# Gated embedding of a decoder layer: where the second half's operand sums stand, which engine adds the residual, and which PSUM banks take the transposes

## The chip, the cores and the metric

The kernel runs on one core of a Trainium2 chip. Its engines are TensorE (PE in the profile, with its weight loads as PEld), VectorE (DVE), ScalarE (ACT), GpSimd (POOL) and SyncE (SP), which here issues every transfer of tiles. The metric is the device time of one execution in microseconds. The trace is one profiled execution.

## The reference, cut to what matters

One layer of a decoder on a sequence of 2048 tokens of width 1024: two kinds of mixing, an output projection, a gated feed-forward part, and at the end a gated embedding. The change touches only the passage from the feed-forward part to the gated embedding and the gated embedding itself:

```
        y = (jax.nn.silu(gate) * up) @ w_down[i]
        h = h + rmsnorm(y, ffn_post_norm[i])
        h = h + (p[i] @ ple_proj[i]) * jax.nn.sigmoid(h @ ple_gate[i])
    return h
```

All arithmetic is float32. Each operand of a product is split into a rounded high part and a low rest, and each product is three matrix products of these (high by high, high by low, low by high).

## The kernel before, in words

The 2048 tokens are handled as four groups of 512 (g = 0 to 3) and, in the last part of the kernel, as two halves of two groups each. Six stages follow each other there: stage 0 `gate_up` of the first half, stage 1 `down` of the first half, stage 2 `gate_up` of the second half, stage 3 `down` of the second half, stage 4 `ple` (the gated embedding) of the first half, stage 5 `ple` of the second half. Every stage computes its matrix product by seven products of sums of blocks, taken in the order 1, 2, 6, 3, 7, 5, 4 (`CHAIN`); `chain` adds each product from its PSUM bank into running sums.

A `ple` stage has 36 steps. Steps 0 to 27 are the seven products of `h @ ple_gate`, four steps each (one for each 128 tokens), twelve matmuls of 512 columns a step. Steps 28 to 35 are `run_p`: for each 128 tokens and each half j of the columns, six matmuls give `p @ ple_proj`; ScalarE takes the sigmoid of the finished sums, VectorE multiplies (L1131), the residual is loaded (L1133) and added (L1134), and the result is stored (L1136).

`pair_of` splits an operand: ScalarE casts the high part (L811), GpSimd or VectorE subtracts it to get the low part (L812). The raw operand lies in one of 12 buffers (`wr`) that `load` (L796) takes in turn for everything. The weights of a step are prepared up to five steps ahead. `Drive` runs the steps in order, and after step i of stage a it calls the functions hung there with `at(a, i, ...)`:

- `s_part(1, ss1, part, k)`, k = 0 to 3, builds the operands of stage 5 from the transposed result. Part 0 makes the operands of products 1, 2 and 6. Part 1 makes those of products 4, 3, 7 and 5: four loads, four additions or subtractions on VectorE (L816, L819), four splits, of which two low parts are on GpSimd (products 4 and 5) and two on VectorE (3 and 7). In the kernel before, part 1 hangs after steps 26, 27, 28 and 29 of stage 4.
- `post_y(g, i)` normalises 128 rows of group g and adds the residual; `turn_y(g, i, tag)` transposes them with TensorE, four 128x128 blocks to a PSUM bank for each half j of the columns (L1086), copies the bank out with ScalarE (L1088) and stores it. Groups 0 and 2 turn in stages 1 and 3 with the tag "mm", groups 1 and 3 in stages 2 (after steps 2 to 5) and 4 (after steps 4 to 7) with the tag "hg".

The PSUM banks have five tags: "mm" has three banks, "z" two, "av", "tr" and "hg" one each. In stages 2, 4 and 5 the products take the tags in the order mm, z, mm, z, mm, av, tr; "hg" is not among them.

The order of TensorE's instructions is that of the program. The order on the other engines and on the transfer queue is made by a planner that simulates the program and takes what it finds ready, earlier program lines first; an engine then runs its own list strictly in order.

Of the kernel before, what the change touches and what calls it, by code (L numbers as in the profile page):

```python
# [89 lines left out]
def hybrid_block(  # L90
# [83 lines left out]
    def bank(tag):  # L174
        return ps.tile([P, 512], F32, tag=tag, name=tag, bufs=BANKS[tag])
# [4 lines left out]
    def mm_bank():  # L180
        mm_count[0] += 1
        return bank(mm_tags[mm_count[0] % len(mm_tags)])
# [40 lines left out]
    def mm3(o, l, r, start, stop):  # L223
        nc.tensor.matmul(o, l[0], r[0], start=start, stop=False)  # L224
        nc.tensor.matmul(o, l[0], r[1], start=False, stop=False)  # L225
        nc.tensor.matmul(o, l[1], r[0], start=False, stop=stop)  # L226

    def cut(pair, j):
        return pair[0][:, j * P:(j + 1) * P], pair[1][:, j * P:(j + 1) * P]
# [564 lines left out]
    def load(src, shape=None):  # L794
        r = slot("wr", 0, "wr")
        nc.sync.dma_start(r if shape is None else shape(r), src)  # L796
        return r

    def acc(name="acc"):
        turns["acc"] += 1  # L800
        return slot("acc", 0 if turns["acc"] % 3 == 0 else 1, name)

    def pair_of(src, kind, prod, lo_engine):
        if kind == "u":
            side = 0 if prod in (1, 2, 6) else 1
        else:
            turns["w"] += 1
            side = turns["w"] % 2
        hi = slot(kind + "h", side, kind + "h", F32R)
        lo = slot(kind + "l", side, kind + "l", F32R)  # L810
        nc.scalar.copy(hi, src)  # L811
        lo_engine.tensor_tensor(lo, src, hi.bitcast(F32), op=ALU.subtract)  # L812
        return hi, lo

    def sub(e, o, a, b):
        e.tensor_tensor(o, a, b, op=ALU.subtract)  # L816

    def add(e, o, a, b):
        e.tensor_tensor(o, a, b, op=ALU.add)  # L819

    V, G = nc.vector, nc.gpsimd
# [65 lines left out]
    def s_blk(grp, i, j, k):  # L887
        return load(h2t_s[2 * grp + i][4 * j + k])
# [15 lines left out]
    def s_part(grp, ss, part, k):  # L904

        a11, a12, a21, a22 = (s_blk(grp, i, j, k) for i, j in ((0, 0), (0, 1), (1, 0), (1, 1)))
        if part == 0:
            ss[1, k] = pair_of(a11, "u", 1, G)
            ss[2, k] = pair_of(a12, "u", 2, V)
            add(V, a21, a21, a22)  # L910
            sub(V, a21, a21, a11)
            ss[6, k] = pair_of(a21, "u", 6, V)
        else:
            ss[4, k] = pair_of(a22, "u", 4, G)
            add(V, a22, a21, a22)
            sub(V, a21, a11, a21)
            sub(V, a11, a22, a11)
            sub(V, a12, a12, a11)
            for prod, a, e in ((3, a12, V), (7, a21, V), (5, a22, G)):
                ss[prod, k] = pair_of(a, "u", prod, e)  # L920

    def chain(prod, c, b, new):

        if prod == 1:
            c["u"] = new("cu")
            nc.scalar.copy(c["u"], b)
        elif prod == 2:
            c[1, 1] = new("c11")
            add(V, c[1, 1], b, c["u"])
        elif prod == 6:  # L930
            add(V, c["u"], b, c["u"])
        elif prod == 3:
            c[1, 2] = new("c12")
            add(V, c[1, 2], b, c["u"])
        elif prod == 7:
            add(V, c["u"], b, c["u"])
        elif prod == 5:
            add(V, c[1, 2], b, c[1, 2])
            c[2, 2] = new("c22")
            add(V, c[2, 2], b, c["u"])  # L940
        else:
            c[2, 1] = c["u"]
            sub(V, c[2, 1], c["u"], b)
# [137 lines left out]
    def turn_y(g, i, tag):  # L1081

        for j, t in enumerate(ready[g][i]):
            b = bank(tag)
            for c in range(TT):
                nc.tensor.transpose(b[:, c * P:(c + 1) * P], t[:, c * P:(c + 1) * P], ident)  # L1086
            e = acc("ht")
            nc.scalar.copy(e, b)  # L1088
            nc.sync.dma_start(
                h2t_s[g][TT * j:TT * (j + 1), :, i * P:(i + 1) * P].rearrange("k p t -> p k t"),  # L1090
                e.rearrange("p (k t) -> p k t", k=TT))


    def ple(grp, ss):
        g0 = 2 * grp
        s = {}
        cs = [{} for _ in range(TT)]
        nk = ND // 2

        def prepare(prod):  # L1100
            w = []
            for k in range(nk):
                if prod in (1, 2, 3):
                    i, j = {1: (0, 0), 2: (1, 0), 3: (1, 1)}[prod]
                    r = (4 * i + k) * P
                    t = load(ple_gate[r:r + P, j * GT:(j + 1) * GT])
                else:
                    t = load(wp_s[k][{5: 1, 6: 2, 7: 3, 4: 4}[prod] - 1])
                w.append(pair_of(t, "w", 0, V if k % 2 else G))
            s[prod] = w  # L1110

        def run(prod, i):
            b = mm_bank()
            for k in range(nk):
                mm3(b, cut(ss[prod, k], i), s[prod][k], k == 0, k == nk - 1)
            chain(prod, cs[i], b, new_dn)

        def prepare_p(half):
            if half == 0:
                s["p"] = [[pair_of(load(ple_proj[k * P:(k + 1) * P, j * GT:(j + 1) * GT]), "w", 0, G)  # L1120
                           for k in range(2)] for j in range(2)]
            s["pt", half] = [pair_of(load(pt_s[g0 + half][k]), "w", 0, V) for k in range(2)]

        def run_p(half, i):
            for j in range(2):
                b = mm_bank()
                for k in range(2):
                    mm3(b, cut(s["pt", half][k], i), s["p"][j][k], k == 0, k == 1)
                y = cs[i][1 + half, 1 + j]
                nc.scalar.activation(y, y, AF.Sigmoid)  # L1130
                nc.vector.tensor_tensor(y, b, y, op=ALU.mult)  # L1131
                c = slice(j * GT, (j + 1) * GT)
                hr = load(h2_s[g0 + half][i * P:(i + 1) * P, c])  # L1133
                add(G, y, y, hr)  # L1134
                r0 = (g0 + half) * GT + i * P
                nc.sync.dma_start(out[r0:r0 + P, c], y)  # L1136

        def none():
            pass

        steps = []
        for pre, go, items in ((prepare, run, CHAIN), (prepare_p, run_p, range(2))):
            for it in items:
                for i in range(TT):
                    steps.append(((lambda pre=pre, it=it: pre(it)) if i == 0 else none,
                                  lambda go=go, it=it, i=i: go(it, i)))
        return steps
# [85 lines left out]
    tt0, tt1, ss0, ss1 = {}, {}, {}, {}  # L1233
# [51 lines left out]
    def at(stage, step, f):  # L1285
        hooks.setdefault((stage, step), []).append(f)
# [24 lines left out]
    for g in range(NG):  # L1311
        stage, step, every, lag, tag = (
            (1, 67, 2, 3, "mm"), (2, 0, 1, 2, "hg"), (3, 67, 2, 3, "mm"), (4, 0, 1, 4, "hg"))[g]
        for i in range(TT):
            at(stage, step + i * every, lambda g=g, i=i: post_y(g, i))
        for i in range(TT):
            at(stage, step + i * every + lag, lambda g=g, i=i, tag=tag: turn_y(g, i, tag))
    for k in range(ND // 2):
        at(4, 13 + 2 * k, lambda k=k: s_part(1, ss1, 0, k))
        at(4, 26 + k, lambda k=k: s_part(1, ss1, 1, k))  # L1320
    drive.run(hooks)


# [25 lines left out]
```

## Time and profile before

| | |
|---|---|
| time, median of 3 runs | 3057.65 us (3057.45 to 3063.77) |
| time of the profiled execution | 3053.19 us |
| span of the profiled execution | 3051.3 us |
| mean granted TensorE clock | 0.988 of full speed |
| busy share of the span | PE 96%, PEld 80%, DVE 68%, ACT 52%, POOL 48% |

The profiled execution's time is the span and 1.9 us around it. All times of the trace count from the start of the span. Stage 2 begins at about 2163 us, stage 4 at 2825 us, its steps 28 to 35 end at 2935.8 us where stage 5 begins, and the last matmul ends at 3046.3 us.

### The profile page before, as it was taken

The page shows a single profiled execution, that of the slowest core. Times are in us where ns is not written, and L with a number is a line of the kernel's source. Part 1 is how long each engine was busy: PE and PEld are TensorE (multiplying, and loading weights), DVE is VectorE, ACT ScalarE, POOL GpSimd, SP SyncE. Part 2 cuts the span into 40 slices and gives each one's busy share as a digit, 9 for nine tenths or more (in the row PEclk, how much of TensorE's full clock was granted, in tenths as well). Part 3 has the DMA queues.
Part 4 walks back from the last instruction along what each step waited for, and adds up shares of the span by engine and source line. Part 5 has one row for each costly group of instructions (what it writes and reads, how often), then busy time and mean ns, then how long its engine had stood idle before and what let it go on. Part 6 is the DMA issues. An engine that isn't in the chain of part 4 may idle for free.

```text
span 3051.3 us, 52890 instructions
## 1 busy us (share of the span) xinstructions
PE 2926.5 (96%) x18280; PEld 2431.2 (80%) x18280; DVE 2071.6 (68%) x2917; ACT 1582.7 (52%) x3188; POOL 1468.2 (48%) x1426
## 2 busy tenths in 40 slices
PE   8999899999999998898898999999999999999989
PEld 6888688878787787788786878888788888878767
DVE  3556566677676776765787787655777776656674
ACT  5666656666666666666523233455433333545442
POOL 3344445545556666867522322445722321457564
PEclk9999999999999999999999999999999999999999
DMA  7775565555545444457867867667955555677874
GB/s 218 220 211 163 151 178 162 149 154 163 151 130 158 144 136 134 153 190 256 285 209 242 265 210 249 224 199 216 342 178 169 173 172 173 210 217 247 308 248 138
DMA packets 469420, 602.28 MB, mean 197 GB/s; under 512 B 43168, under 2 KB 277664, under 8 KB 469152
## 3 DMA queue, kind: packets, MB, share of 16 engines
q1 hardware_dynamic: 469152, 598.91, 62.6%
q8 instruction: 144, 2.36, 0.3%
q14 instruction: 124, 1.02, 0.1%
HBM read 439.89 MB, written 158.86 MB: 196 GB/s over the span
## 4 chain that ended last, share of the span: by engine, by line
PE 43%; DVE 3%; DMA 3%; POOL 2%; issue 2%; ACT 1%; SPq 0%; POOLq 0%; DVEq 0%; ACTq 0%
PE mm L224 6%; PE mm L225 6%; PE mm L226 6%; PE z L226 4%; PE z L225 4%; PE z L224 4%; PE av L225 2%; PE av L226 2%; PE tr L224 2%; PE tr L225 2%; PE tr L226 2%; PE av L224 2%; DMA wr<-in_w_gate_up_dram 1%; DVE wl L812 1%; DVE wr L816 1%
## 5 line engine op out<-in xcount | busy, mean ns | idle before, releaser
L811 ACT CAST wh<-wr 128x512 fp32r<-128x512 f32 x600 | 352.1, 618 | 458.1 <-PE mm L225 159.9
L812 POOL TENSOR_TENSOR wl<-wr,wh 128x512 fp32r<-128x512 f32 x256 | 370.5, 1453 | 452.7 <-ACT wh L811 437.7
L435 POOL TENSOR_TENSOR a<-be,ring 128x512 f32<-128x512 f32 (+2 forms) x320 | 318.1, 994 | 436.0 <-DVE ring L431 418.9
L224 PE MATMUL mm<-uh,wh 128*128 128x512 f32 x1168 | 486.5, 417 | 3.5 <-DVE vv L350 2.0
L226 PE MATMUL mm<-uh,wl 128*128 128x512 f32 x1168 | 462.6, 396 | 0.0
L225 PE MATMUL mm<-ul,wh 128*128 128x512 f32 x1168 | 460.6, 394 | 0.0
L812 DVE TENSOR_TENSOR wl<-wr,wh 128x512 fp32r<-128x512 f32 x344 | 302.0, 885 | 182.9 <-ACT wh L811 172.5
L431 DVE TENSOR_TENSOR_SCAN ring<-z,ring,be 128x512 f32<-128x512 f32 x192 | 245.6, 1279 | 115.3 <-ACT z L417 112.3
L224 PE MATMUL mm<-wh,uh 128*128 128x256 f32 (+1 forms) x992 | 308.0, 310 | 0.0
L225 PE MATMUL mm<-wl,uh 128*128 128x256 f32 (+1 forms) x992 | 293.4, 296 | 6.9 <-POOL wl L812 6.9
L226 PE MATMUL mm<-wh,ul 128*128 128x256 f32 (+1 forms) x992 | 293.4, 296 | 0.0
L226 PEld LDWEIGHTS mm<-uh,wl 128*128 128x128 f32 x1168 | 221.5, 190 | 51.4
L224 PEld LDWEIGHTS mm<-uh,wh 128*128 128x128 f32 x1168 | 222.8, 191 | 46.2 <-issue 2.1
L225 PEld LDWEIGHTS mm<-ul,wh 128*128 128x128 f32 x1168 | 223.1, 191 | 39.9
L448 DVE TENSOR_TENSOR al<-tr,ah 128x512 fp32r<-128x512 f32 (+1 forms) x320 | 192.1, 600 | 90.7 <-ACT ah L446 90.0
L210 ACT CAST wh<-wr 128x512 fp32r<-128x512 f32 x288 | 178.3, 619 | 136.6 <-PE mm L225 80.8
L211 POOL TENSOR_TENSOR wl<-wr,wh 128x512 fp32r<-128x512 f32 x144 | 189.8, 1318 | 104.1 <-ACT wh L210 95.7
L812 POOL TENSOR_TENSOR wl<-s,wh 128x512 fp32r<-128x512 f32 x44 | 101.0, 2300 | 279.5 <-ACT wh L811 255.4
L446 ACT CAST ah<-tr 128x512 fp32r<-128x512 f32 (+1 forms) x320 | 167.5, 524 | 110.9 <-PE tr L443 108.2
L416 ACT ACTIVATE be<-z 128x512 f32<-128x512 f32 (+2 forms) x320 | 171.0, 534 | 88.2 <-PE z L410 38.5
L225 PEld LDWEIGHTS mm<-wl,uh 128*128 128x128 f32 x992 | 191.4, 193 | 12.5 <-POOL wl L812 7.4
L224 PEld LDWEIGHTS mm<-wh,uh 128*128 128x128 f32 x992 | 191.1, 193 | 7.9
(310 smaller groups left out, 7269.2 us busy)
## 6 DMA issues: line engine op xcount, KB each, us to landing
wr<-in_w_gate_up_dram SPq DMA_DIRECT2D x308, 256.0 KB, 3.8
wr<-in_w_in_dram SPq DMA_DIRECT2D x224, 256.0 KB, 3.2
wr<-hid_s SPq DMA_DIRECT2D x154, 256.0 KB, 3.1
wr<-in_w_down_dram SPq DMA_DIRECT2D x110, 256.0 KB, 3.4
hid_s<-hs SPq DMA_DIRECT2D x88, 256.0 KB, 3.7
wr<-wd_s SPq DMA_DIRECT2D x88, 256.0 KB, 3.1
kt<-k_s SPq DMA_DIRECT2D x80, 256.0 KB, 3.0
vt<-v_s SPq DMA_DIRECT2D x80, 256.0 KB, 3.3
```

Of the source, the lines that this page charges most:

```text
L210: nc.scalar.copy(hi, src)
L211: (lo_engine or nc.gpsimd).tensor_tensor(lo, src, hi.bitcast(F32), op=ALU.subtract)
L224: nc.tensor.matmul(o, l[0], r[0], start=start, stop=False)
L225: nc.tensor.matmul(o, l[0], r[1], start=False, stop=False)
L226: nc.tensor.matmul(o, l[1], r[0], start=False, stop=stop)
L416: nc.scalar.activation(be[:, :n], z[:, :n], AF.Sigmoid, scale=0.125)
L431: nc.vector.tensor_tensor_scan(r[:, o:o + n][:, ::-1], z[:, :n][:, ::-1], be[:, :n][:, ::-1], init, op0=ALU.mult, op1=ALU.bypass)
L435: nc.gpsimd.tensor_tensor(a[:, :n], be[:, :n], r[:, o + 1:o + n + 1], op=ALU.mult)
L446: nc.scalar.copy(hi[:, lo_c:], tr[:, lo_c:])
L448: nc.vector.tensor_tensor(lo[:, lo_c:], tr[:, lo_c:], hi[:, lo_c:].bitcast(F32), op=ALU.subtract)
L811: nc.scalar.copy(hi, src)
L812: lo_engine.tensor_tensor(lo, src, hi.bitcast(F32), op=ALU.subtract)
```

## The change

Three edits. `turn_y` takes the bank for the first half of the columns (j = 0) from the tag "mm" in every group, and only the second half uses the tag it was given; so groups 1 and 3 turn over an "mm" and the "hg" bank by turns, and nothing changes for groups 0 and 2. In `run_p` the residual of the first half of the columns (j = 0) is added on VectorE, that of the second stays on GpSimd. Part 1 of `s_part` for the second half is hung after steps 0, 2, 4 and 6 of stage 5 instead of steps 26 to 29 of stage 4.

```diff
     def turn_y(g, i, tag):
 
         for j, t in enumerate(ready[g][i]):
-            b = bank(tag)
+            b = bank(tag if j else "mm")
             for c in range(TT):
                 nc.tensor.transpose(b[:, c * P:(c + 1) * P], t[:, c * P:(c + 1) * P], ident)
...
                 hr = load(h2_s[g0 + half][i * P:(i + 1) * P, c])
-                add(G, y, y, hr)
+                add(G if j else V, y, y, hr)
...
     for k in range(ND // 2):
         at(4, 13 + 2 * k, lambda k=k: s_part(1, ss1, 0, k))
-        at(4, 26 + k, lambda k=k: s_part(1, ss1, 1, k))
+        at(5, 2 * k, lambda k=k: s_part(1, ss1, 1, k))
```

## Rows read from the trace of the kernel before

**Rows 1.** The page: busy us of each engine (share of the span).

```profile
PE 2926.5 (96%) x18280; PEld 2431.2 (80%) x18280; DVE 2071.6 (68%) x2917; ACT 1582.7 (52%) x3188; POOL 1468.2 (48%) x1426
```

**Rows 2.** Waits of PE from 2170 us on: total us, times, longest us.

```profile
PE hg L1086 <- ACT ht L1088: 7.1, 7, 2.5
PE mm L225 <- POOL wl L812: 6.9, 1, 6.9
PE mm L226 <- DVE wl L812: 2.4, 2, 2.1
...
PE hg L1086 <- POOL wl L812: 0.8, 1, 0.8
```

**Rows 3.** Timeline of PE, group 1 turned in stage 2: start us, us, instructions.

```profile
2180.15 0.60 PE L1086 MATMUL hg<-ident,cu 128*128 128x128 f32 x4
...
2181.90 0.47 PE L224 MATMUL z<-uh,wh 128*128 128x512 f32 x1
...
2202.32 0.60 PE L1086 MATMUL hg<-ident,cu 128*128 128x128 f32 x4
...
2205.79 0.47 PE L224 MATMUL mm<-uh,wh 128*128 128x512 f32 x1
2206.10 0.58 PE L225 MATMUL mm<-ul,wh 128*128 128x512 f32 x1
...
2209.75 0.39 PE L225 MATMUL mm<-ul,wh 128*128 128x512 f32 x1
2209.98 0.40 PE L226 MATMUL mm<-uh,wl 128*128 128x512 f32 x1
```

**Rows 4.** Timeline of PE: a turn of group 2 ("mm"), one of group 3 ("hg").

```profile
2803.45 1.04 PE L1086 MATMUL mm<-ident,c 128*128 128x128 f32 x8
2804.25 0.47 PE L224 MATMUL z<-wh 128*128 128x512 f32 x1
...
2838.97 0.60 PE L1086 MATMUL hg<-ident,cu 128*128 128x128 f32 x4
...
2840.72 0.48 PE L224 MATMUL mm<-wh,uh 128*128 128x512 f32 x1
```

**Rows 5.** Timeline of DVE in stage 2: the sum that frees an "mm" bank.

```profile
2187.00 0.68 DVE L819 TENSOR_TENSOR cu<-mm,cu 128x512 f32<-128x512 f32 x1
```

**Rows 6.** Timeline of PE in step 0 of stage 5.

```profile
2937.21 0.40 PE L224 MATMUL mm<-wh,uh 128*128 128x512 f32 x1
2944.55 0.79 PE L225 MATMUL mm<-wl,uh 128*128 128x512 f32 x1 [6.94 <-POOL wl L812]
...
2950.26 0.40 PE L226 MATMUL av<-wh,ul 128*128 128x512 f32 x1
```

**Rows 7.** Granted clock by stretch: PE, PEld, DVE, ACT, POOL busy; PEclk, DMA.

```profile
2945.00:2951.00 6.00, 6.00 (x17) 4.61 (x17) 1.03 (x2) 1.62 (x3) 6.00 (x5) 0.56 1.03 379
```

**Rows 8.** Timeline of POOL at the border of stages 4 and 5.

```profile
2934.80 2.99 POOL L819 TENSOR_TENSOR c<-c,wr 128x512 f32<-128x512 f32 x2 [0.68 <-DVE wr L819]
...
2942.78 1.72 POOL L812 TENSOR_TENSOR wl<-wr,wh 128x512 fp32r<-128x512 f32 x1
```

**Rows 9.** Groups of DVE from 2896 to 2945 us: busy us, mean ns.

```profile
L812 DVE TENSOR_TENSOR ul<-wr,uh 128x512 fp32r<-128x512 f32 x8 | 11.5, 1457 | 0.5 <-ACT uh L811 0.4
L816 DVE TENSOR_TENSOR wr<-wr 128x512 f32<-128x512 f32 x12 | 11.4, 952 | 0.1
L812 DVE TENSOR_TENSOR wl<-wr,wh 128x512 fp32r<-128x512 f32 x6 | 5.0, 846 | 0.0
L819 DVE TENSOR_TENSOR wr<-wr 128x512 f32<-128x512 f32 x4 | 3.8, 950 | 4.9 <-POOL ul L812 4.9
```

**Rows 10.** Timeline of DVE: the first sum of part 1.

```profile
2896.75 0.69 DVE L819 TENSOR_TENSOR wr<-wr 128x512 f32<-128x512 f32 x1 [2.80 <-POOL ul L812]
```

**Rows 11.** Timelines at the end: the last matmul of PE, POOL's last add.

```profile
3045.87 0.39 PE L226 MATMUL av<-wh,wl 128*128 128x512 f32 x1
...
3047.07 1.26 POOL L819 TENSOR_TENSOR c<-c,wr 128x512 f32<-128x512 f32 x1
```

## Prediction

> **What bounds the kernel now.** I read the page first, then the waits of PE, then PE's timeline around each wait. TensorE is busy for 96% of the span [rows 1], so time comes off only where TensorE stands still or works slowly. The waits of PE from stage 2 on show where it stands [rows 2]. Three of them lie in the places that the diff touches: it waits for ScalarE's copy of a transposed bank (7.1 us in seven turns, and 0.8 us in the eighth, where the profile names GpSimd but the place is the same), for one low part of a weight on GpSimd (6.9 us, once), and for a low part on VectorE (2.4 us) at the first steps of `run_p`. Each is small against 3000 us, and with TensorE full everywhere else a microsecond taken from one of them should reach the end.
>
> **The transposes.** In groups 1 and 3 both halves of the columns use the single "hg" bank: four transposes, then TensorE waits until ScalarE has emptied it, then four more. In group 1 a turn takes 1.75 us from its first transpose to the next matmul, and the last one 3.47 us [rows 3]; the other two of group 1 are like the first. In group 3 it is 1.75 us each [rows 4]. Group 2 turns over several "mm" banks, eight transposes without a stop, and takes 0.80 us [rows 4]. The changed code gives the two halves two different banks, so I price a turn at 0.80 us. Group 1: 3 x 1.75 + 3.47 - 4 x 0.80 = 5.5 us. Group 3: 4 x (1.75 - 0.80) = 3.8 us. The number of transposes and copies stays.
>
> The long stop of 3.47 us has a second price. After it nine matmuls take from 2206.10 to 2209.75, 3.65 us, where the following one shows 0.23 us for each [rows 3]: 3.65 - 9 x 0.23 = 1.6 us. It looks like the lower of TensorE's two clock levels, as the granted clock shows at the border below. Without the stop this should go: 1.6 us.
>
> What it adds is a wait for an "mm" bank. There are three, the products use three of every seven tags on them, and four more tenants come in. Behind a waiting transpose stands every later matmul. The one place where I find the bank late is the second turn of group 1: VectorE frees the bank of the third step at 2187.00 + 0.68 = 2187.7 us [rows 5], and the second turn, due at about 2187.5 us now (5.6 us after 2181.90, two products on), would come 0.95 us earlier, at 2186.6. If the banks go strictly round, that costs 1.1 us; if the free one is taken, nothing. The bounds for all eight turns are 0 and 8 x 1.1; I take 1.1 us, since in stage 4 VectorE is not behind and I find no late bank there.
>
> **The border of stages 4 and 5.** In the first step of stage 5 TensorE waits 6.9 us for the low part of the third weight, on GpSimd [rows 6]. GpSimd was not idle: from 2934.80 us it ran five residual adds, and the low part came behind them at 2942.78 us [rows 8]. These adds were late because VectorE was: from 2896 to 2945 us it spent 11.4 + 3.8 us on the 16 sums of part 1 and 11.5 us on their eight low parts, 26.7 of 49 us [rows 9], and the products that GpSimd was to add to stood between them. The change takes both away: the 26.7 us go to stage 5, and 8 of the 16 adds of each half leave GpSimd. VectorE gets 8 adds at 0.69 to 0.95 us [rows 9, 10], at most 8 us in place of the 26.7. GpSimd then has one add of at most 1.7 us [rows 8] for each 2.8 us step, so it should meet the weight in time: 6.9 us go. After the stop, 13 matmuls take from 2944.55 to 2950.26, 5.71 us [rows 6]; at 0.23 us they would take 3.0. The granted clock of that stretch is 0.56 of full [rows 7], mostly the lower level. Without the stop another 2.7 us go.
>
> The 2.4 us that TensorE waits for VectorE at the start of `run_p` [rows 2] are for the low parts of `p`, which stood among the same sums. With these gone I count 2.4 us; bounds 0 and 2.4.
>
> **What moves into stage 5.** All of part 1 goes with its 16 loads, 16 casts, 16 sums and 16 low parts. On the transfer queue the loads move past the residual loads and the stores of stage 4's `run_p`, and stand among the weights of products 6 and 3. Its first result is needed at step 12 (product 3), and all four k are needed there. A step is 12 x 0.23 = 2.8 us, so from the end of step 0, behind which the first sum is written, there are 11 steps or 30.4 us. VectorE's list for that stretch: part 1 at its old lengths 26.7 us, less the last low part of product 7 (1.46), eight sums of products 2 and 6 at 0.68 us [rows 5] = 5.4, six low parts of weights at 0.85 us [rows 9] = 5.1; together 35.8 us. That is 5.4 us too much if nothing starts early. But the planner takes work early where an engine is free: the first sum of part 1 ran at 2896.75 us [rows 10], while the step behind which it is written ended some ten steps of 2.8 us before 2937, at about 2909. In the changed stage 4 a `run_p` step leaves VectorE 2.8 - 2 x 0.68 - 0.8 = 0.6 us free, some 5 us over eight steps. So the operands come just in time or slightly late; I take 1 us, with bounds 0 and 5.4 + 2.7 for a stop long enough to lower the clock.
>
> A new wait sits inside this: the first sum of each k may overwrite its input only after GpSimd has made the low part of product 4, 2.80 us in the row [rows 10]. Behind it on VectorE stand the sums that free PSUM banks. A product's bank comes round after at least two steps, 5.6 us, so one such wait does not reach TensorE.
>
> A rule speaks against both moves. By the Trainium skill, "SBUF — State Buffer", section "Who interferes with whom", a VectorE instruction with two SBUF inputs and a GpSimd instruction that reads SBUF exclude each other for the whole instruction. The rows agree that there is a price: the sums of part 1 mean 0.95 us beside GpSimd's work, and 0.69 us for the first one [rows 9, 10]; what full exclusion would cost is a rival below.
>
> **The end.** The last matmul ends at 3046.3 us and GpSimd's last add starts at 3047.07 [rows 11]. It belongs to the second half of the columns and stays on GpSimd, so the tail is unchanged. If VectorE's add of the first half falls beside it, it takes 1.72 instead of 1.26 us [rows 8, 11]: 0 to +0.5 us, I take 0. The eight adds that VectorE now makes in stage 5 lie under matmuls: VectorE needs 2 x 0.68 + 0.8 = 2.2 us of a step's 2.8; if that cover went, it would be 8 x 0.7 us.
>
> **Sum.** Gains 5.5 + 3.8 + 1.6 + 6.9 + 2.7 + 2.4 = 22.9 us; losses 1.1 + 1.0. Net 20.8 us. Against the profiled execution's own 3053.19 us (span 3051.3 and 1.9 around it) that is 3032.4; the median of the runs lies 4.5 us above that execution, and from it the forecast is 3057.65 - 20.8 = 3037 us.
>
> **Rivals.**
> 1. VectorE late in stage 5. For it: the list of 35.8 us in 30.4, and the VectorE wait of [rows 10]. Against it: the free time before. If nothing starts early, 5.4 us of stop and 2.7 of clock: 22.9 - 1.1 - 8.1 = 13.7 us gained, 3044 us.
> 2. The border's stop survives, because GpSimd still has eight adds and part 1's first low parts may be drawn ahead of the weight. It keeps 9.6 us: 20.8 - 9.6 = 11.2 gained, 3046 us. Against it: what fed the queue, VectorE's 26.7 us, has left.
> 3. Full exclusion of VectorE and GpSimd. Alone, VectorE's list of stage 5 is 38 instructions (24 of part 1, eight sums, six low parts) at 0.68 us = 25.8 us; GpSimd's 14 low parts (eight of part 1, six of weights) at 1.26 us add 17.6. 43.4 against 30.4 us is 13 us of stop and 2.7 of clock: 22.9 - 1.1 - 15.7 = 6 us gained, 3052 us, about no change. This is what the rule of the Trainium skill ("SBUF — State Buffer") would give. Against it: 0.95 us is far below 0.68 + 1.26. The same result comes if the planner's new order opens stops elsewhere.
> 4. Slower: the raw buffers. Part 1 needs 16 loads, and the 12 `wr` buffers are shared with the weights taken ahead. If the planner loads the weights of products 6 and 3 first, part 1 runs only from the end of step 7, four steps or 11 us before it is needed, and before it was spread over 48 us [rows 9, 10]. 48 - 11 = 37 us of stop and 2.7 of clock against 21.8 gained: 18 us slower, 3076 us. It decides from a stop of 19 us on. Against it: the casts of those weights free their buffers as the earlier products finish, and part 1's first three k are written before the weights of product 3.
>
> **How the numbers follow.** Forecast 0.52; rival 1 0.20; rival 2 0.12; rival 3 and other new orders 0.09; rival 4 0.07. A change of 0.2% (6 us) is about what a measurement of this kernel can tell from none. The first three are faster by more than that: 0.84; rival 3 is the same: 0.09; rival 4 slower: 0.07. The forecast's own range is 3033 to 3041 from the bounds above (0 and 2.2 us of loss, 0 or 2.4 for `p`); the runs' scatter, 4.5 us down to the profiled one, takes its lower end to 3029. With rivals 1 and 2 the upper end is 3049, which leaves 0.16 out.
>
> **What would show it.** Right: turns of groups 1 and 3 in 0.8 us; no PE wait for L1088; no stop at the first step of stage 5 and no stretch of 0.43 us matmuls behind it; last add 2 us after the last matmul. Wrong: a PE wait at step 12 of stage 5 for a low part on VectorE (rival 1 or 3, by its length), a PE wait for GpSimd in step 0 (rival 2), loads of the second half's operands issued only after step 7 (rival 4), transposes waiting for VectorE (the banks).

## The result, and the profile after

The kernel after takes 3042.06 us (median of 4 runs, 3038.41 to 3045.58), the kernel before, in the same comparison, 3059.99 us (median of 4, 3057.45 to 3063.77). The ratio is 0.995 with a 95% interval of 0.9932 to 0.9967: 15 us faster, 10 to 21 by the interval (the two medians lie 17.9 us apart). The forecast was 3037 us in a range of 3029 to 3049. The profiled execution took 3042.35 us with a span of 3040.5 us.

The page of the kernel after, busy us of each engine, answers to [rows 1]:

```profile
PE 2925.5 (96%) x18280; PEld 2431.2 (80%) x18280; DVE 2082.0 (68%) x2933; ACT 1580.9 (52%) x3188; POOL 1459.0 (48%) x1410
```

VectorE has the sixteen residual sums that GpSimd has lost (x2933 for x2917, x1410 for x1426). Otherwise no engine has more or less to do, and what changed are the waits. The waits of PE of the kernel after from 2170 us on (total us, times, longest us) answer to [rows 2]:

```profile
PE mm L224 <- ACT uh L811: 9.6, 2, 9.1
PE z L226 <- DVE wl L812: 1.4, 1, 1.4
PE mm L1086 <- POOL c L819: 1.2, 1, 1.2
PE hg L1086 <- POOL c L819: 0.5, 1, 0.5
```

All three waits of [rows 2] on which the forecast rested are gone: the one for ScalarE's copy of the bank, the 6.9 us for GpSimd, the one for the low parts of `p`. One stands there that was not in the kernel before: 9.6 us for a high part from ScalarE.

The order of TensorE's instructions is the same in both kernels, so the path can be cut at the same instructions and the parts compared. The cuts, in the timeline of PE of the kernel after (start us, us, instruction): the first transpose of group 0, the first of group 1, the matmul behind group 1's last turn, the first transpose of group 2, the matmul behind group 3's last turn, `run_p` of stage 4, stage 5, its step 12, its step 14, its `run_p`, the last matmul.

```profile
2141.96 1.03 PE L1086 MATMUL mm<-ident,c 128*128 128x128 f32 x8
2178.81 0.60 PE L1086 MATMUL mm<-ident,cu 128*128 128x128 f32 x4
2199.66 0.48 PE L224 MATMUL mm<-uh,wh 128*128 128x512 f32 x1
2795.69 1.04 PE L1086 MATMUL mm<-ident,c 128*128 128x128 f32 x8
2843.31 0.47 PE L224 MATMUL z<-wh,uh 128*128 128x512 f32 x1
2899.11 0.40 PE L224 MATMUL mm<-wh 128*128 128x512 f32 x1
2921.59 0.39 PE L224 MATMUL mm<-wh,uh 128*128 128x512 f32 x1
2955.01 0.40 PE L224 MATMUL mm<-wh,uh 128*128 128x512 f32 x1
2973.79 0.39 PE L224 MATMUL mm<-wh,uh 128*128 128x512 f32 x1
3012.78 0.39 PE L224 MATMUL mm<-wh 128*128 128x512 f32 x1
3035.02 0.39 PE L226 MATMUL av<-wh,wl 128*128 128x512 f32 x1
```

Differences of these starts, and the same differences in the kernel before, whose cuts start at 2143.29, 2180.15, 2205.79, 2803.45, 2854.62, 2910.43, 2935.82, 2979.04, 2984.61, 3023.63 and 3045.87 us:

| stretch | before, us | after, us | change |
|---|---|---|---|
| group 0 to group 1 | 36.86 | 36.85 | 0.0 |
| turns of group 1 (stage 2) | 25.64 | 20.85 | -4.8 |
| from there to group 2 | 597.66 | 596.03 | -1.6 |
| groups 2 and 3 (stages 3, 4) | 51.17 | 47.62 | -3.6 |
| to `run_p` of stage 4 | 55.81 | 55.80 | 0.0 |
| `run_p` of stage 4 | 25.39 | 22.48 | -2.9 |
| stage 5, steps 0 to 11 | 43.22 | 33.42 | -9.8 |
| stage 5, steps 12 and 13 | 5.57 | 18.78 | +13.2 |
| stage 5, steps 14 to 27 | 39.02 | 38.99 | 0.0 |
| its `run_p` to the last matmul | 22.24 | 22.24 | 0.0 |
| all | 902.58 | 893.06 | -9.5 |

So between the two profiled executions the changed passage gave 9.5 us, not the 20.8 of the forecast: 22.7 us came off and 13.2 were put back in two steps. Another 1.3 us lie in the code ahead of group 0's transposes, which the change does not touch and in which every engine runs the same list: it ends at 2143.3 us in the one profiled execution and at 2142.0 in the other, and in the twelve other traces of this study, in which it is the same too, between 2143.9 and 2151.5. The ratio of whole runs carries this scatter. That it makes up all the rest of the 15 us is not shown, as the other executions left no trace; the same two kernels measured again (below) differ by 6 us, 2 to 10. The cut times are free of that scatter, and I rest on them below, but each is of one execution.

The turns, in the timeline of PE of the kernel after, answer to [rows 3] and [rows 4]: the first two of group 1, and the first of group 3.

```profile
2178.81 0.60 PE L1086 MATMUL mm<-ident,cu 128*128 128x128 f32 x4
2179.95 0.66 PE L1086 MATMUL hg<-ident,c 128*128 128x128 f32 x4 [0.54 <-POOL c L819]
2180.36 0.47 PE L224 MATMUL z<-uh,wh 128*128 128x512 f32 x1
...
2186.01 0.60 PE L1086 MATMUL mm<-ident,cu 128*128 128x128 f32 x4
...
2186.80 0.48 PE L224 MATMUL z<-uh,wh 128*128 128x512 f32 x1
...
2831.56 0.60 PE L1086 MATMUL mm<-ident,cu 128*128 128x128 f32 x4
2832.35 0.48 PE L224 MATMUL mm<-wh,uh 128*128 128x512 f32 x1
```

A turn takes 0.79 us in both groups (2186.80 - 2186.01, 2832.35 - 2831.56), but for the very first, where the second half waits 0.54 us for the residual sum on GpSimd. No transpose waits for a bank: the second turn starts at 2186.01 and goes through. VectorE ends the third step's sum, which frees the "mm" bank that the forecast expected to be late, only at 2186.2.

The new stop, in the timeline of PE of the kernel after, is in step 12 of stage 5, the first of product 3:

```profile
2957.15 0.50 PE L224 MATMUL mm<-wh,uh 128*128 128x512 f32 x1 [0.58 <-ACT uh L811]
...
2967.43 0.79 PE L224 MATMUL mm<-wh,uh 128*128 128x512 f32 x1 [9.05 <-ACT uh L811]
...
2973.14 0.58 PE L225 MATMUL z<-wl,uh 128*128 128x512 f32 x1
```

Behind it 13 matmuls take from 2967.43 to 2973.14, 5.71 us: the very stretch that stood behind the stop of [rows 6], 2.7 us more than at full pace. The granted clock over it, in the windows of the kernel after (busy us of PE, PEld, DVE, ACT, POOL; clock, DMA share, GB/s), is 0.50, the lower of the two levels, as it is in the kernel before over the same stretch (2944.55 to 2950.26 us; the 0.56 of [rows 7] takes in 0.75 us behind it):

```profile
2968.00:2973.00 5.00, 5.00 (x13) 3.87 (x12) 1.40 (x3) 0.42 (x1) 1.35 (x1) 0.50 0.62 201
```

ScalarE is only the last link. Its timeline in the kernel after shows the sixteen casts of part 1 in five bundles, and what it waited for:

```profile
2927.84 0.62 ACT L811 CAST uh<-wr 128x512 fp32r<-128x512 f32 x1
...
2933.93 2.18 ACT L811 CAST uh<-wr 128x512 fp32r<-128x512 f32 x4
...
2944.95 2.18 ACT L811 CAST uh<-wr 128x512 fp32r<-128x512 f32 x4
...
2956.48 2.18 ACT L811 CAST uh<-wr 128x512 fp32r<-128x512 f32 x4 [3.67 <-DVE wr L816]
...
2966.76 1.66 ACT L811 CAST uh<-wr 128x512 fp32r<-128x512 f32 x3 [6.02 <-DVE wr L816]
```

A bundle of four is products 3, 7 and 5 of one set and product 4 of the next. The last bundle waits 6.02 us for the sums of the fourth set on VectorE. The timeline of DVE of the kernel after, first sum of each set and the last sums:

```profile
2929.86 0.69 DVE L819 TENSOR_TENSOR wr<-wr 128x512 f32<-128x512 f32 x1 [1.88 <-POOL ul L812]
...
2941.59 0.68 DVE L819 TENSOR_TENSOR wr<-wr 128x512 f32<-128x512 f32 x1
...
2951.41 0.68 DVE L819 TENSOR_TENSOR wr<-wr 128x512 f32<-128x512 f32 x1
...
2961.26 1.74 DVE L819 TENSOR_TENSOR wr<-wr 128x512 f32<-128x512 f32 x1
2962.93 1.75 DVE L812 TENSOR_TENSOR wl<-wr,wh 128x512 fp32r<-128x512 f32 x1
2964.60 2.13 DVE L816 TENSOR_TENSOR wr<-wr 128x512 f32<-128x512 f32 x3
```

The sets start 10 to 12 us apart, although they are written two steps, 5.6 us, apart. The fourth ends at 2964.60 + 2.13 = 2966.73 us; step 12 stands at 2955.01. The experiments ask why.

### The profile page after: what moved, and what is told of

It reads as the page before. It is cut to its first block, busy times and chain, and to the rows that moved or that the text cites. A ratio compares the mean times of both kernels' runs of the same rounds, so it can differ in the third digit from the quotient of the medians.

```text
span 3040.5 us, 52870 instructions
## 1 busy us (share of the span) xinstructions
PE 2925.5 (96%) x18280; PEld 2431.2 (80%) x18280; DVE 2082.0 (68%) x2933; ACT 1580.9 (52%) x3188; POOL 1459.0 (48%) x1410
## 4 chain that ended last, share of the span: by engine, by line
PE 40%; issue 4%; DVE 3%; DMA 3%; POOL 3%; ACT 1%; SPq 0%; POOLq 0%; DVEq 0%; ACTq 0%
PE mm L224 5%; PE mm L225 5%; PE mm L226 5%; PE z L226 4%; PE z L225 4%; PE z L224 4%; PE av L225 2%; PE av L224 2%; PE av L226 2%; PE tr L224 2%; PE tr L226 2%; PE tr L225 2%; POOL wl L812 1%; DVE wl L812 1%; DMA wr<-in_w_gate_up_dram 1%
## 5 line engine op out<-in xcount | busy, mean ns | idle before, releaser
L226 PEld LDWEIGHTS mm<-uh,wl 128*128 128x128 f32 x1168 | 220.6, 189 | 51.3 <-POOL wl L211 0.3
L224 PEld LDWEIGHTS mm<-wh,uh 128*128 128x128 f32 x992 | 192.5, 194 | 18.4 <-ACT uh L811 10.4
```

## The experiments

Each table row below is the same cut of a profiled execution as above: the turns of group 1, groups 2 and 3, `run_p` of stage 4, steps 0 to 11 and steps 12 and 13 of stage 5, and all from group 0's first transpose to the last matmul, in us. The ratio is that of whole runs to the runs of the kernel before beside them, with its 95% interval.

| kernel | group 1 | groups 2, 3 | `run_p` | 0 to 11 | 12, 13 | all | ratio |
|---|---|---|---|---|---|---|---|
| before | 25.6 | 51.2 | 25.4 | 43.2 | 5.6 | 902.6 | 1 |
| after | 20.9 | 47.6 | 22.5 | 33.4 | 18.8 | 893.1 | 0.995 (0.9932 to 0.9967) |
| banks alone | 21.1 | 48.6 | 26.9 | 39.7 | 5.6 | 893.1 | 0.9968 (0.9958 to 0.9979) |
| residual sums alone | 24.9 | 51.3 | 25.6 | 42.5 | 5.6 | 900.0 | 1.0003 (0.9992 to 1.0014) |
| operand sums alone | 25.3 | 51.3 | 22.5 | 33.8 | 17.6 | 900.9 | 0.9992 (0.9979 to 1.0004) |
| banks and residual sums | 21.1 | 47.7 | 27.0 | 41.1 | 5.6 | 894.3 | 0.9985 (0.9976 to 0.9995) |
| after, once more | 21.0 | 48.4 | 22.5 | 33.4 | 18.4 | 894.1 | 0.998 (0.9967 to 0.9992) |
| product 7's low part on GpSimd | 21.0 | 47.4 | 22.5 | 33.4 | 18.9 | 893.5 | 0.9975 (0.9961 to 0.9989) |
| product 4's low part on VectorE | 21.1 | 47.5 | 22.5 | 33.4 | 16.5 | 891.0 | 0.9965 (0.9953 to 0.9978) |
| part 1 half a stage earlier | 20.8 | 47.4 | 22.5 | 45.3 | 5.6 | 892.0 | 0.9966 (0.9954 to 0.9977) |
| first sum into its own buffer | 21.2 | 48.5 | 22.5 | 33.4 | 8.3 | 883.8 | 0.9955 (0.9937 to 0.9973) |
| and product 4 split last | 21.1 | 48.3 | 22.5 | 33.4 | 8.0 | 886.0 | 0.9954 (0.9939 to 0.9969) |
| product 4's operand apart | 21.0 | 47.3 | 22.5 | 33.4 | 5.6 | 881.0 | 0.9931 (0.9907 to 0.9955) |
| that, residual sums on GpSimd | 21.1 | 47.3 | 22.5 | 33.8 | 5.6 | 880.8 | 0.9927 (0.9914 to 0.9941) |

### The three edits, one by one

**Banks alone.** The kernel before with

```diff
-            b = bank(tag)
+            b = bank(tag if j else "mm")
```

> Only the banks of the transposes are changed. My theory (the three edits act on separate stops): the eight turns of groups 1 and 3 fall from 1.75 to 3.5 us to 0.8 us, and the 1.6 us of slow matmuls in stage 2 go: 9 to 11 us faster, with the 6.9 us stop at the border of stages 4 and 5 unchanged. Rival (time won early is lost again at the next full engine): the border stop grows by what the turns give, and the kernel is faster by less than 4 us.

The two rows of turns fall by 4.6 and 2.5 us, and the kernel is 9.4 us faster by the cut times and 10 by the ratio, as expected. The stop at the border did not stay as it was: with nothing edited there, the waits of PE of this kernel show 3.3 us, half of its 6.9 us [rows 2].

```profile
PE mm L225 <- POOL wl L812: 3.3, 1, 3.3
```

Little of that is a gain. Steps 0 to 11 are 3.6 us shorter, but `run_p` is 1.5 us longer and the stretch ahead of it 0.9 (56.7 for 55.8): over the whole border, 1.2 us. TensorE comes earlier and waits at other places. The 0.9 are mostly a wait of 0.8 us for a high part from ScalarE ahead of the first matmul of `run_p`. In `run_p` the wait for VectorE is as long as before (2.3 us for 2.4), but behind it the granted clock falls: 0.66 from 2911 to 2916 us, where the kernel before shows 1.00 from 2911 to 2918.

**Residual sums alone.** The kernel before with

```diff
-                add(G, y, y, hr)
+                add(G if j else V, y, y, hr)
```

> Only the residual adds of the first half of the columns go to VectorE. My theory (VectorE, with 26.7 us of part 1 between its products, is what makes GpSimd's adds late): VectorE gets eight more instructions in the same stretch, so the border stop stays within 3 us of its 6.9 us; between 4 us faster and 4 us slower. Rival (GpSimd's queue of adds is the cause): with half the adds gone the low part of the weight is in time, the stop and the slow matmuls behind it vanish, 8 to 10 us faster.

The waits of PE of this kernel: the one stop has become two, and `p` is as late as before.

```profile
PE mm L225 <- POOL wl L812: 2.9, 1, 2.9
PE mm L226 <- DVE wl L812: 2.6, 2, 2.4
PE mm L225 <- DVE wl L812: 2.3, 1, 2.3
```

`run_p` and steps 0 to 11 together go from 68.6 to 68.1 us. By itself this edit moves the lateness from GpSimd to VectorE and gives nothing that runs can tell.

**Operand sums alone.** The kernel before with

```diff
-        at(4, 26 + k, lambda k=k: s_part(1, ss1, 1, k))
+        at(5, 2 * k, lambda k=k: s_part(1, ss1, 1, k))
```

> Only part 1 of the operand sums is moved to stage 5. My theory: the border stop and the 2.4 us wait for the low parts of p go (12 us with the slow matmuls), and the stop at product 3 of stage 5 seen in the changed kernel (9.6 us and 2.5 us of slow matmuls) comes: between 3 us faster and 3 us slower. Rival (the stop at product 3 comes from VectorE's extra adds or from the shifted arrival of TensorE, not from the sums): no stop at product 3, 10 to 12 us faster.

The border is as in the kernel after, 22.5 and 33.8 us: this edit alone takes both the stop and the wait for `p`, 12.3 us. And this edit alone makes the stop at product 3, as the waits of PE of this kernel show:

```profile
PE mm L224 <- ACT uh L811: 9.0, 1, 9.0
```

12.0 us are given back in steps 12 and 13. The edit as it stands is worth 0.3 us.

**Banks and residual sums**, the first two edits together.

> Banks and adds are changed, part 1 stays in stage 4. My theory: no stop at product 3 of stage 5; the turns give 9 to 11 us and the border stop stays in about the size that the adds alone leave it. Rival (GpSimd's queue is the cause of the border stop): 18 to 21 us faster than before, thus faster than the changed kernel.

The turns are as with the banks alone. Over the border (56.9 + 27.0 + 41.1 us for 55.8 + 25.4 + 43.2) it is 0.5 us slower than before. While the operand sums are in stage 4, the border as a whole moves by 1.2 us at most. By the ratio of whole runs this kernel gains 5 us and the banks alone 10, while their passages differ by 1.1 us; the rest of that difference is not explained.

### The stop at product 3: how long the list, or in what order?

**The kernel after once more**, beside the next three.

> The changed kernel once more, beside the next three. Expected as before: 12 to 18 us faster than the kernel before, with a stop of 8 to 11 us at product 3 of stage 5, before which TensorE waits for the cast of the fourth operand, and one stretch of slow matmuls behind it. If the stop is an accident of one execution, it is absent here.

The stop is 9.6 us again, with 18.4 us in steps 12 and 13: no accident of one execution. Its ratio, 0.998, means 6 us (2 to 10), below the 12 to 18 expected and below the 15 of the first comparison. Its cut time from group 0 on is only 1.0 us longer: the passage is worth 8.5 to 9.5 us, and the two ratios, from 4 and from 10 runs of the kernel after, lie on either side of that.

**Product 7's low part on GpSimd**: four instructions fewer on VectorE between the border and product 3.

```diff
-            for prod, a, e in ((3, a12, V), (7, a21, V), (5, a22, G)):
+            for prod, a, e in ((3, a12, V), (7, a21, G), (5, a22, G)):
```

> As the changed kernel, but the four low parts for product 7 are made on GpSimd instead of VectorE. Theory 1 (VectorE's list before step 12 is too long): three to four instructions of 0.7 to 1.7 us leave it, the stop at product 3 falls from 9.6 to 4 to 6 us; 3 to 6 us faster than the changed kernel. Theory 2 (VectorE waits in the chain from ScalarE's cast over GpSimd's low part for product 4 to the first sum, and is not full): GpSimd has four more instructions in that chain, the stop stays or grows by up to 5 us.

The stop is 10.5 us (the waits of PE of this kernel):

```profile
PE mm L224 <- ACT uh L811: 10.5, 2, 9.5
```

Taking work from VectorE did not shorten it. That speaks against a list too long for its time as the only cause, but the four low parts went to GpSimd, which the other theory has in the chain, so it does not decide between them.

**Product 4's low part on VectorE**: four instructions more there, and no wait for GpSimd ahead of the first sum.

```diff
-            ss[4, k] = pair_of(a22, "u", 4, G)
+            ss[4, k] = pair_of(a22, "u", 4, V)
```

> As the changed kernel, but the four low parts for product 4 are made on VectorE instead of GpSimd, so the first sum of each k no longer waits for GpSimd. Theory 1 (VectorE's list is too long): four instructions more, the stop at product 3 grows by 2 to 6 us. Theory 2 (the chain over GpSimd makes it late): the stop shrinks by 3 us or more.

The stop is 8.3 us, against 9.6 (the waits of PE of this kernel):

```profile
PE mm L224 <- ACT uh L811: 8.3, 1, 8.3
```

More work on VectorE, and 1.3 us less of a stop. That is not what a list too long would do, but it is less than the 3 us or more that the removal of the wait on GpSimd was to bring. It settled neither.

**Part 1 half a stage earlier**: its four parts hung after steps 30, 32 and 34 of stage 4 and step 0 of stage 5.

```diff
-        at(5, 2 * k, lambda k=k: s_part(1, ss1, 1, k))
+        at(*((4, 30), (4, 32), (4, 34), (5, 0))[k], lambda k=k: s_part(1, ss1, 1, k))
```

> As the changed kernel, but part 1 of the four sets hangs after steps 30, 32 and 34 of stage 4 and step 0 of stage 5. Theory 1 (VectorE's list between the end of step 0 and step 12 is too long): some 14 us more of time, the stop at product 3 vanishes; with the residual adds halved the border stop stays below 3 us: 8 to 13 us faster than the changed kernel. Rival (any sums in stage 4 bring the border stop back, whatever their number): a stop of 3 to 7 us for a weight's low part in step 0 of stage 5, within 5 us of the changed kernel.

Nothing stands at product 3, but steps 0 to 11 take 45.3 us, more than before the change. The waits of PE of this kernel name low parts of weights on both engines:

```profile
PE z L225 <- DVE wl L812: 4.0, 2, 2.7
PE mm L225 <- POOL wl L812: 2.0, 1, 2.0
```

The place in the program shifts the stop; it does not remove it. The passage is 1.1 us shorter than in the kernel after; the rival had said within 5 us.

### Cutting the chain

What these leave is a chain of orders. In the in-place sums, the first writes `a22 + a21` over `a22`, which product 4's split still reads. So in each set: ScalarE's cast for product 4, GpSimd's low part, the first sum, three more sums, the casts for products 3, 7 and 5, and behind these, in ScalarE's list, the next set's cast for product 4. The bundles above show it. For the fourth set in the kernel after: product 4's cast ends at 2956.48 + 2.18 = 2958.66; GpSimd's low part follows, in its timeline:

```profile
2958.22 2.57 POOL L812 TENSOR_TENSOR ul<-wr,uh 128x512 fp32r<-128x512 f32 x2 [4.25 <-ACT uh L811]
```

It ends at 2960.79, and the first sum starts at 2961.26; the last ends at 2966.73, and ScalarE casts at 2966.76. Some 10 us for one round, with what VectorE does in between (the weight's low part at 2962.93), four rounds in a row: from 2927.84, the first cast, to 2966.76 are 38.9 us, and from the border to step 12 there are 33.4.

**First sum into its own buffer.** The kernel after with a raw buffer more for each set; VectorE's list keeps its length.

```diff
-            add(V, a22, a21, a22)
+            add(V, n := slot("wr", 0, "wr"), a21, a22)
             sub(V, a21, a11, a21)
-            sub(V, a11, a22, a11)
+            sub(V, a11, n, a11)
             sub(V, a12, a12, a11)
-            for prod, a, e in ((3, a12, V), (7, a21, V), (5, a22, G)):
+            for prod, a, e in ((3, a12, V), (7, a21, V), (5, n, G)):
```

> The changed kernel, but the first sum of each set of part 1 is written to a raw buffer of its own, so that it need not wait until GpSimd has made the low part of product 4. VectorE's list keeps its length and ScalarE's casts their program order. Theory 1 (the list of VectorE between the border and product 3 is too long): the stop at product 3 stays at 8 to 10 us. Theory 3 (a chain in each set, cast of product 4, its low part on GpSimd, the first sum, the casts of products 3, 7 and 5, then the next set, some 10 us each and four of them in a row): the sums of the four sets start close together, the stop is gone or at most 3 us, and the kernel is 9 to 12 us faster than the changed one.

The waits of PE of this kernel:

```profile
PE mm L225 <- POOL wl L812: 0.7, 1, 0.7
PE mm L224 <- ACT uh L811: 0.5, 1, 0.5
```

The stop is 0.5 us, and 0.7 us for a weight beside it; steps 12 and 13 take 8.3 us for 18.8, with small gaps only. VectorE had the same instructions to do as in the kernel after, so 10.5 of the 13.2 us came from the one buffer that is written over. What is left goes with a full list. The windows from the border to the end of the last sum, of the kernel after and of this kernel (busy us of PE, PEld, DVE, ACT, POOL; clock, DMA share, GB/s):

```profile
2921.59:2966.73 45.14, 36.20 (x154) 28.43 (x152) 38.89 (x41) 19.79 (x36) 25.14 (x17) 0.92 0.70 234
2927.64:2964.39 36.75, 35.98 (x154) 28.35 (x152) 35.77 (x36) 17.29 (x32) 23.95 (x15) 1.00 0.73 243
```

In the kernel after VectorE is busy for 38.9 of 45.1 us and idle for 6.2. Here it is idle for 1.0, and three low parts of weights have moved behind the last sum. It has no room left, and the last sum still ends 3.3 us behind the place of step 12 (36.75 - 33.43). Nor do the four sets start close together, as theory 3 had it: their first sums start 6, 12, 23 and 28 us behind the border.

**And product 4 split last**, so that ScalarE casts for products 3, 7 and 5 first. As above, with

```diff
-            ss[4, k] = pair_of(a22, "u", 4, G)
...
-            for prod, a, e in ((3, a12, V), (7, a21, V), (5, n, G)):
+            for prod, a, e in ((3, a12, V), (7, a21, V), (5, n, G), (4, a22, G)):
```

> As the run with the sum's own buffer, and the split for product 4 is written last in each set, so that ScalarE casts for products 3, 7 and 5 first. Theory 1: a stop of 8 to 10 us as in the changed kernel. Theory 3 with the overwritten buffer as the only link of the chain: the same as with the own buffer alone, within 1 us. Theory 3 with ScalarE's order as a second link: the stop is at least 1 us shorter than with the own buffer alone, or is gone where that one still shows 1 to 3 us.

8.0 us in steps 12 and 13, the same within 0.3: the stop for ScalarE is 0.5 us in both. Once the buffer is free, ScalarE's order costs nothing more. (This execution is 2.2 us longer from group 0 to group 1, which has nothing to do with the edit; that is why its sum, 886.0, stands above that of the run before it.)

**Product 4's operand apart.** Part 1 makes only the sums and products 3, 7 and 5; product 4's block is loaded once more and split later.

```diff
-            ss[4, k] = pair_of(a22, "u", 4, G)
...
         at(5, 2 * k, lambda k=k: s_part(1, ss1, 1, k))
+        at(5, 8 + 2 * k, lambda k=k: ss1.update({(4, k): pair_of(s_blk(1, 1, 1, k), "u", 4, G)}))
```

> The changed kernel, but part 1 makes only the sums and the operands of products 3, 7 and 5; the operand of product 4 is loaded once more and split after steps 8, 10, 12 and 14 of stage 5 (four loads of 256 KB more). VectorE's list until product 3 is as long as before. Theory 1: the stop at product 3 stays at 8 to 10 us. Theory 3: it is gone or at most 2 us, and the kernel is 9 to 12 us faster than the changed one, unless the low parts of product 4 now come late at step 24, which would show as a wait for GpSimd there.

No wait at product 3 and none at product 4. The timeline of DVE of this kernel, first sums of the first, second and fourth set and the last sum of all:

```profile
2938.84 0.69 DVE L819 TENSOR_TENSOR wr<-wr 128x512 f32<-128x512 f32 x1 [0.21 <-DMA wr<-h2t_s]
...
2942.13 0.69 DVE L819 TENSOR_TENSOR wr<-wr 128x512 f32<-128x512 f32 x1 [0.41 <-DMA wr<-h2t_s]
...
2955.56 0.68 DVE L819 TENSOR_TENSOR wr<-wr 128x512 f32<-128x512 f32 x1
...
2961.39 0.68 DVE L816 TENSOR_TENSOR wr<-wr 128x512 f32<-128x512 f32 x1
```

The sums no longer wait for GpSimd; the first two wait for their loads. In this execution the border is at 2932.24 us, so the last sum ends 29.8 us behind it (2961.39 + 0.68 - 2932.24), 3.6 us ahead of step 12. In the kernel after it ended 45.1 us behind (2966.73 - 2921.59). The whole passage takes 881.0 us, 21.6 less than before, and the ratio is lower than both of the kernel after: 0.9931 against 0.998 and 0.995, though its interval overlaps that of the latter.

**That kernel with the residual sums back on GpSimd.**

```diff
-                add(G if j else V, y, y, hr)
+                add(G, y, y, hr)
```

> The kernel with product 4's operand apart, but without the edit on the residual sums: all sixteen of each half on GpSimd, as before. It asks what the residual sums on VectorE are worth once the operand sums have left stage 4. Theory A (the sums of part 1 alone kept GpSimd's list late at the border): no stop at the first step of stage 5 and none at product 3, within 2 us of the kernel with product 4's operand apart, some 20 us below before. Theory B (GpSimd's sixteen sums are themselves too many): a wait for a low part of a weight on GpSimd comes back in the first steps of stage 5 or at product 3, and 3 to 7 us of the gain are lost.

880.8 us, and 0.9927. Steps 0 to 11 take 33.8 us for 33.4; nothing else differs. The waits of PE of this kernel from 2170 us on, all of them:

```profile
PE z L226 <- DVE wl L812: 1.3, 1, 1.3
PE mm L1086 <- POOL c L819: 1.1, 1, 1.1
PE hg L1086 <- POOL c L819: 0.8, 1, 0.8
```

With the operand sums out of stage 4, GpSimd has time for all sixteen sums. By the cut times the edit on the residual sums is worth 0.4 us.

## Why the forecast came out, and where it did not

- **Turns of group 1, 5.5 us forecast:** 4.8. Turns of 0.79 us as priced, and a 0.54 us wait of the first for GpSimd's residual sum, which the stop on the bank had covered.
- **Turns of group 3, 3.8 us:** 4 x (1.75 - 0.79) = 3.8.
- **Slow matmuls in stage 2, 1.6 us:** 1.6 in the two profiled executions (597.66 and 596.03 us), but the two kernels that still turn over "hg" alone show 596.2 and 596.1 us there. Their last turns wait 1.7 and 2.2 us on the bank, where the kernel before waited 2.5, and the granted clock stays at 1.00 behind them. The slow matmuls belonged to that one execution, and the banks' own worth is the 7 to 8 us of the two rows of turns (4.6 + 2.5 with the banks alone, 4.8 + 3.6 in the kernel after).
- **A late "mm" bank, 1.1 us lost:** 0. Of the two cases, the free bank was the right one: the second turn started 0.2 us before VectorE was done with the late one.
- **Stop at the border and the slow matmuls behind it, 6.9 + 2.7 us:** 9.8 gained, for the reason given (VectorE's sums held up what feeds GpSimd). But nearly all of it is the operand sums' work; the residual sums, which I named beside them, have 0.4 us of it (33.8 and 33.4 us).
- **Low parts of `p`, 2.4 us:** 2.9, the whole of `run_p`.
- **The tail:** unchanged. From the end of the last matmul to the end of the span are 5.0 us before (3051.3 - 3046.3) and 5.1 after (3040.5 - 3035.4).
- **The step that failed** is "So the operands come just in time or slightly late; I take 1 us". It cost 13.2 us: 9.6 of waiting, 2.7 of lower clock behind it, and 0.9 in small gaps around the first wait. No sum started early: the first ran 8.3 us after the border (2929.86 - 2921.59), not before it.

Rival 1, VectorE late in stage 5, named the place, but its 5.4 + 2.7 us are 5 us short of the 13.2. Its cause, a list of 35.8 us in 30.4, is one part of the answer: VectorE is busy for 38.9 us between the border and the last sum, more than the 33.4 there are up to step 12, and 2.7 us of the loss stayed when the chain was cut. The larger part, 10.5 us, went with one buffer more and the same instructions. It stood in the prediction, as "a new wait sits inside this". I priced it by what is queued behind it on VectorE and found PSUM banks in time. I did not follow it the other way round, from one set to the next: four such rounds stand in a row, because the casts of one set are queued ahead of the next set's first cast on ScalarE. In the kernel before this chain had stood too [rows 10], spread over some 48 us in which nobody waited for it.

Rival 2 (the border's stop survives) came true in the kernels with the operand sums still in stage 4, with stops of 2.0 to 3.3 us, and nowhere else. Rival 4 did not occur: in the kernel after, the loads of part 1 were all issued by 2941.9 us, within step 7, and the kernel that takes five raw buffers for each set in place of four was faster, not slower. Rival 3 had the nearest price for this place, 13 + 2.7 us, and its mechanism is in the rows. Beside GpSimd's work a sum of two tiles takes 1.74 us in place of 0.68 (the first sums of the fourth and the third set above), and GpSimd's own low part alone takes 1.30. By the Trainium skill, "SBUF — State Buffer", section "Who interferes with whom", a VectorE instruction with two SBUF inputs and a GpSimd instruction that reads SBUF exclude each other for a whole instruction. The trace comes near that: full exclusion of these two would make 0.68 + 1.30, and 1.74 was measured. It did not hold for the whole list, which the forecast of no change needed: in the groups of DVE from 2921.6 to 2966.7 us the nine low parts of weights have a mean of 1.60 us, the six of operands 1.16, but the twelve other sums 0.69. As an estimate, the 41 instructions of the window above would take 28 us at 0.68 each; they took 38.9, so working beside GpSimd cost VectorE some 11 us.

The forecast of whole runs, 3037, is 5 us below the median, which lies inside the range, but that is in part luck: on the passage itself 9.5 us stand against 20.8, and the same two kernels measured again differ by 6 us. On the passage rivals 1 to 3 (13.7, 11.2 and 6 us) came nearer than the forecast.

What stays open: why part 1 was not taken earlier (the first load was issued at 2918.51 us, some 6 us ahead of its place in the program, and the first cast ran 3 us behind that place, where in the kernel before the first sum ran some ten us ahead of it); and why the code ahead of group 0, the same everywhere, takes between 2142.0 and 2151.5 us.

## What to carry to other kernels

When work is moved nearer to its use, don't only add up the lists of the engines against the time left: write down one round of the work, link by link through all engines, with what is overwritten in place, and multiply it by the rounds that follow each other. A link that cost nothing where there was time becomes the bound where there is none, and one buffer more can cut it; then the list is the next bound. And price each edit of a change alone: here one edit gave all of its 7 to 8 us, one took 12 and gave 12 back, and one gave nothing.

## What the runs showed of the hardware

- Behind a stop of 9.05 us, and of 6.94 us in the kernel before [rows 6], the slow stretch has the same length: 13 matmuls in 5.71 us, at a granted clock of 0.50 in both. Waits of about 2 us went either way: behind one of 2.5 us in stage 2 the clock fell (0.53 over the nine slow matmuls of [rows 3]), behind those of 1.7 and 2.2 us at the same place in two other kernels it stayed at 1.00. Gaps of 0.5 to 0.8 us have no slow stretch behind them: the windows of the kernel with the first sum in its own buffer show 1.00 around its two short waits.

```profile
2962.00:2967.00 5.00, 4.15 (x13) 2.39 (x14) 5.00 (x7) 2.58 (x5) 2.68 (x3) 1.00 0.63 188
```

- On VectorE a sum or difference of two SBUF tiles (128x512 float32) takes 0.68 us, and up to 1.80 beside GpSimd's work (the latter in the kernel with the first sum in its own buffer, at 2957.50 us). A sum with one input in a PSUM bank takes 0.68 beside it too (in the kernel after at 2958.34 us, while GpSimd works from 2958.22 to 2960.79).
- Code that is the same in all kernels of the study took 2142.0 to 2151.5 us in the fourteen traces, more of a difference than some edits are worth. Cut times repeat within 0.1 us where nothing waits (22.24 to 22.25 us from `run_p` of stage 5 to the last matmul, in all fourteen). The row of groups 2 and 3 scatters by 1.4 us among kernels with the same banks; the last turn of group 2 waits for GpSimd in all of them.
